# A hybrid layer with 32 experts on one core: expert weights as 2 MB pieces of a pair, in blocks of 4,096 columns, with 11 slots instead of 14

## The chip, the cores and the metric

The kernel runs on one core of a Trainium2 chip. The metric is device time in microseconds (us) of one execution; the time given is the median of several. The engines are TensorE (PE, its weight loads PEld), VectorE (DVE), ScalarE (ACT), GpSimd (POOL) and SyncE (SP); in this kernel SP issues all DMAs, and 16 DMA engines carry them out. TensorE's granted clock was 0.986 of full speed over the span.

## The reference

One layer over 256 tokens of width 1024, batch 1, all in float32. Four mixers of width 512 read one wide projection; then come the expert layer and the PLE branch, each with a layer norm after it.

```
z = x @ w_in                                  # zA, zB, zC, zD and the gates zG
yA, yB, yC, yD = rwkv7_mix(zA), hgrn2_mix(zB), mlstm_mix(zC), rglru_mix(zD)
merged = sum over n of sigmoid(zG)[n] * (y_n @ w_branch[n])
x = layernorm(alpha * x + merged @ w_out)
top_val, top_idx = top_k(x @ router_w + router_b, 4);  gate = softmax(top_val)
for each of the 32 experts, on its tokens:
    gu = x @ w_gu[e] + b_gu[e];  gate_, up = gu[:, :1024], gu[:, 1024:]       # clipped
    y  = ((up + 1) * gate_ * sigmoid(1.702 * gate_)) @ w_down[e] + b_down[e]
moe = sum of y * gate
ple = sigmoid(x @ ple_gate_w) * (p @ ple_proj_w)
out = layernorm(alpha * x + moe + ple)
```

The weights of the experts are 32 x (1024 x 2048 + 1024 x 1024) floats, 403 MB of the 475 MB that the kernel moves.

## The kernel before

The first 435 us (the front) hold the projection, the four mixers, the output projection, the first layer norm and the router. Then comes the expert stage: the experts are taken in 16 pairs, and both experts of a pair work in one product, each on one half of the 128 partitions of the output (64 tokens each). For pair `i`, `up(i)` makes the gate and up products (four of 1024 x 512 per expert), with bias, and the swiglu; `down(i, filler)` makes two products of 1024 x 512 per expert; `turn`, `gather`, `combine` and `down_bias` put the small products for transposing, for collecting the tokens of the next two pairs, for adding the result back and for the bias between them. After pairs 4 and 5 `ple(j)` makes one half of the PLE: the gate product with `w_pg` (32 products, L1868) and the projection with `w_pp` (8 products, L1878). Engines run in the order in which the program is written; nothing is reordered.

All weights come through one list, `stream`, in the order of use. `pump()` walks along it and issues as many DMAs on SP as places are free, `chunk()` hands a piece to the product that uses it, and `drop()` gives the place back and calls `pump()` again. A piece is 1 MB: 128 partitions x 2,048 floats, one run of 8,192 bytes per partition, for one expert. It lies in one of two kinds of place:

- a slot, 2,048 columns of its own (`Slots`, NSLOT = 14), used for other things in the front, too;
- a block of the arena (`Arena`, one wide tile of 22,208 columns, from which all other buffers are cut). `ar.blocks()` counts the free blocks of `B` columns (2,048); in the expert stage (`ar.tight`) large pieces start on block borders and small buffers avoid whole blocks.

The number of free places that must be left over is `st["keep"]`: 3, then `KEEP`, then 5 from the second pair on. A DMA that writes over a place waits for the last reader of what lay there, PE for weights; the wait stands on SP, and the DMAs behind it stand behind it. Up to eight DMAs are under way, since the program has eight DMA semaphores in turn. The last pieces of the last pair (`tails`) come in six DMAs with runs of 1,024 bytes or more, so that the end can start on parts.

The pair product, L1699 to L1710, and the lines of `pump()` that place a piece:

```
            if len(sl.idle) > st["slots"]:
                t = sl.get(F32)
                ...
            elif spare > (st["keep"] if st["slots"] else 0):
                ready[key] = al(shape)
```

Of the kernel before, what the change touches and what calls it, by code (L numbers as in the profile page):

```python
# [20 lines left out]
T = 256  # L21
# [106 lines left out]
class Arena:  # L128


    G, B = 32, 2048 // 32

    def __init__(self, t, cols):
        self.t, self.n = t, cols // self.G
        self.used = np.zeros(self.n, bool)
        self.freed = np.zeros(self.n, np.int64)
        self.now, self.live, self.peak, self.tight, self.low = 1, {}, 0, False, False

    def get(self, shape, dt=F32):
# [9 lines left out]
        if self.tight:  # L149
# [3 lines left out]
            else:  # L153
                whole = np.repeat(~self.used[:self.n // B * B].reshape(-1, B).any(axis=1), B)
                whole = np.append(whole, np.zeros(self.n - len(whole), bool))
                w = w + np.where(np.lib.stride_tricks.sliding_window_view(whole, g).any(axis=1), 1 << 40, 0)
        if self.low:
            w = np.where(w < 1 << 60, w >> 40 << 40, w) + np.arange(len(w))
# [43 lines left out]
NSLOT = 14  # L202
# [9 lines left out]
def hybrid_kernel(ctx: ExitStack, tc: tile.TileContext, xT, x, w_in, pc_d, rows_d, cn_d, lv_d, wa2, g2, lrub, w_br,  # L212
# [91 lines left out]
    st = {"next": 0, "out": 0, "ahead": 4, "slots": 1, "keep": 3}  # L304
    LATE = "br2_3"
    tails = [("dn", e, 512, 1) for e in (NE - 2, NE - 1)]

    def want(key, src, shape):
        stream.append((key, src, shape))

    def pump():
        while st["next"] < len(stream):
# [3 lines left out]
            if key in tails:  # L316
                if len(sl.idle) < len(tails):
                    break
                for key, _, shape in stream[st["next"]:]:
                    t = sl.get(F32)  # L320
                    place[key] = (sl.free, t)
                    ready[key] = in_slot(t, shape)
                for cc, k, n in ((0, 0, 4), (256, 0, 2), (256, 2, 2)):
                    for key, src, _ in stream[st["next"]:]:
                        src = src.rearrange("p (k c) -> p k c", k=4)
                        SY.dma_start(ready[key][:, k:k + n, cc:cc + 256], src[:, k:k + n, cc:cc + 256])
                st["next"] = len(stream)
                break
            spare = ar.blocks() if ar.tight else 0
            if st["slots"] == 0 and spare + len(sl.idle) <= st["keep"]:  # L330
                break
            if len(sl.idle) > st["slots"]:
                t = sl.get(F32)
                place[key] = (sl.free, t)
                ready[key] = in_slot(t, shape)
            elif spare > (st["keep"] if st["slots"] else 0):
                ready[key] = al(shape)
                place[key] = (fr, ready[key])
            elif late and st["out"] < 2:
                release(late.pop(0)[1])  # L340
                continue
            else:
                break
            if st["next"] == 0:
# [15 lines left out]
    def drop(key):  # L360
        f, t = place.pop(key)
        f(t)
# [227 lines left out]
    def rwkv():  # L590
# [56 lines left out]
        BK_t = sl.get(F32)  # L647
        BK = in_slot(BK_t, [128, 4, 512]).rearrange("p c (n i s) -> p c n i s", n=4, i=2)
        AR_t = sl.get(F32)
        AR = in_slot(AR_t, [128, 4, 512]).rearrange("p c (n i s) -> p c n i s", n=4, i=2)  # L650
# [77 lines left out]
        BKt_t = sl.get(F32)  # L728
        BKt = in_slot(BKt_t, [128, 4, 512])
# [35 lines left out]
        sl.free(BK_t)  # L765
# [144 lines left out]
        sl.free(AR_t)  # L910
        sl.free(BKt_t)
# [480 lines left out]
    def want_up(i):  # L1392
        for half in ((0, 0), (1, 0), (0, 1), (1, 1)):
            c0 = half[0] * D + half[1] * 512
            for k in range(2):
                for e in (2 * i, 2 * i + 1):
                    want(("gu", e, c0, k), w_gu[e, c0 // 512, k], [128, 4, 512])

    def want_down(i):
        for j in range(2):  # L1400
            for k in range(2):
                for e in (2 * i, 2 * i + 1):
                    want(("dn", e, j * 512, k), w_dn[e, j, k], [128, 4, 512])
        if i in PLE:
            j = PLE.index(i)
            for k in range(2):
                want(("pg", 0, j * 512, k), w_pg[j, k], [128, 4, 512])
# [10 lines left out]
    pump()  # L1418
    lz["pc"] = fetch(pc_d, [128, NPC])
    lz["half"] = al([128, 1])  # L1420
    G.memset(lz["half"], -0.5)
# [732 lines left out]
```

## Time and profile before

| | us |
|---|---|
| median of 3 runs | 1400.31 (1399.62 to 1402.27) |
| profiled execution | 1402.92 |
| its span, first to last instruction | 1400.5 |
| PE busy | 1294.5 (92 %) |
| DVE busy | 504.4 (36 %) |
| ACT busy | 330.6 (24 %) |
| DMA, mean over the span | 339 GB/s, 474.84 MB |

The rows further down come from the profiled execution. Times in them are us from the start of the span; L1705 is line 1705 of the kernel before. "slot", "arena" and "bank" are the names of places (a bank is an accumulator of PE), and in_w_gu, in_w_dn, in_w_pg, in_w_pp, in_w_in, in_w_br, in_w_out the weights in memory.

### The profile page before, as it was taken

Reading aid. Unit: us, or ns where it says so; the run is one execution under the profiler, and the core shown is the slowest. Engines: PE = TensorE matmul, PEld = TensorE weight load, DVE = VectorE, ACT = ScalarE, POOL = GpSimd, SP = SyncE. Lnnn points to the kernel's source line nnn. Section 1 sums busy time; section 2 is a strip of 40 time slices with the busy share of each in tenths; the row PEclk is TensorE's granted clock in tenths of the full one; section 3 lists DMA queues with packets and bytes.
Section 4 is the critical chain, followed back from the end, with each engine's and each line's share of the span. In section 5 each row is a group of like instructions: output and inputs, shape, how many; then the busy total and the mean of one; then the engine's idle time right before and its main releaser. Section 6 shows DMA issues by size and latency. Waiting matters only on the chain. (4 is left out here: it accounts for less than half of the span.)

```text
span 1400.5 us, 17423 instructions
## 1 busy us (share of the span) xinstructions
PE 1294.5 (92%) x7269; PEld 717.8 (51%) x7269; DVE 504.4 (36%) x715; ACT 330.6 (24%) x499; POOL 187.6 (13%) x197
## 2 busy tenths in 40 slices
PE   8988899999999998999889999989988898898985
PEld 8977879999994342333224333423433332342332
DVE  5887876686674122121121212201121211121114
ACT  6765654665433010010001000100100100010000
POOL 0578944413100000000000000000000000000000
PEclk9999999999999999999999999999999999999998
DMA  9413244458566999999999999999999999999995
GB/s 350 156 42 136 91 137 138 148 184 333 201 247 275 422 421 410 421 421 422 421 421 420 417 420 421 421 421 421 421 421 421 420 422 421 422 421 421 422 421 188
DMA packets 80151, 474.84 MB, mean 339 GB/s; under 512 B 14114, under 2 KB 20898, under 8 KB 24388
## 3 DMA queue, kind: packets, MB, share of 16 engines
q1 hardware_dynamic: 80068, 473.68, 83.7%
q8 instruction: 59, 0.97, 0.3%
q14 instruction: 24, 0.20, 0.0%
HBM read 472.07 MB, written 1.57 MB: 338 GB/s over the span
## 5 line engine op out<-in xcount | busy, mean ns | idle before, releaser
L1705 PE MATMUL bank<-slot,arena 128*64 128x512 f32 x2856 | 712.1, 600 | 58.1 <-DMA slot<-in_w_dn 32.1
L1705 PEld LDWEIGHTS bank<-slot,arena 128*64 128x64 f32 x2856 | 224.4, 137 | 460.7 <-issue 326.2
L378 PE MATMUL bank<-slot,slot 128*128 128x256 f32 (+2 forms) x800 | 243.9, 305 | 5.0 <-ACT slot L407 5.0
L379 PE MATMUL bank<-slot,slot 128*128 128x256 f32 (+2 forms) x800 | 239.6, 300 | 2.1 <-DVE slot L374 2.1
L380 PE MATMUL bank<-slot,slot 128*128 128x256 f32 (+2 forms) x800 | 239.7, 300 | 2.0 <-DVE slot L374 2.0
L378 PEld LDWEIGHTS bank<-slot,slot 128*128 128x128 f32 (+1 forms) x800 | 155.1, 194 | 11.7 <-ACT slot L407 5.0
L380 PEld LDWEIGHTS bank<-slot,slot 128*128 128x128 f32 (+1 forms) x800 | 155.1, 194 | 7.0 <-DVE slot L374 2.8
L379 PEld LDWEIGHTS bank<-slot,slot 128*128 128x128 f32 (+1 forms) x800 | 155.2, 194 | 6.2 <-DVE slot L374 2.5
L374 DVE TENSOR_TENSOR slot<-slot,slot 128x1024 fp32r<-128x1024 f32 (+1 forms) x89 | 123.8, 1399 | 47.8 <-ACT slot L373 47.6
L1695 DVE TENSOR_SCALAR arena<-bank 128x512 f32<-128x512 f32 x32 | 22.1, 692 | 236.9 <-PE bank L1705 230.1
L373 ACT CAST slot<-slot 128x1024 fp32r<-128x1024 f32 (+1 forms) x99 | 101.4, 1040 | 13.3 <-DVE slot L374 5.5
L1694 ACT ACTIVATE arena<-arena 128x512 f32<-128x512 f32 x32 | 20.2, 631 | 347.2 <-DVE arena L1693 347.2
L1716 DVE SCALAR_TENSOR_TENSOR slot<-bank,arena,slot 128x512 fp32r<-128x512 f32 (+1 forms) x33 | 24.2, 735 | 209.4 <-ACT slot L1715 209.1
L1581 POOL CAST se<-arena 128x128 fp32r<-128x128 f32 x16 | 5.0, 322 | 670.0 <-PE bank L1588 622.6
L1728 DVE TENSOR_TENSOR arena<-arena,bank 128x512 f32<-128x512 f32 (+1 forms) x66 | 40.1, 667 | 131.0 <-PE bank L1727 131.0
L1715 ACT ACTIVATE slot<-bank,arena 128x512 fp32r<-128x512 f32 (+1 forms) x33 | 22.3, 676 | 264.8 <-PE bank L1705 255.1
L1705 PE MATMUL bank<-arena 128*64 128x512 f32 x184 | 73.3, 599 | 5.4 <-DMA arena<-in_w_dn 2.7
L1693 DVE TENSOR_SCALAR arena<-bank 128x512 f32<-128x512 f32 x32 | 22.1, 689 | 120.6 <-PE bank L1705 120.6
L540 POOL TENSOR_TENSOR arena<-arena 128x4 f32<-128x4 f32 (+2 forms) x10 | 9.8, 990 | 354.7 <-DVE arena L2061 293.2
L1541 ACT ACTIVATE arena<-bank,arena 128x256 f32<-128x256 f32 x36 | 20.1, 566 | 114.1 <-DVE arena L1543 114.1
L1705 PEld LDWEIGHTS bank<-arena 128*64 128x64 f32 x184 | 21.0, 138 | 38.1 <-issue 26.8
L1794 ACT COPY arena<-bank 128x512 f32<-128x512 f32 x32 | 17.2, 590 | 92.3 <-PE bank L1793 92.3
(373 smaller groups left out, 1074.4 us busy)
## 6 DMA issues: line engine op xcount, KB each, us to landing
slot<-in_w_gu SPq DMA_DIRECT2D x237, 1024.0 KB, 18.6
slot<-in_w_dn SPq DMA_DIRECT2D x122, 1024.0 KB, 19.8
slot<-in_w_in SPq DMA_DIRECT2D x38, 1024.0 KB, 4.9
arena<-in_w_gu SPq DMA_DIRECT2D x19, 1024.0 KB, 16.0
slot<-in_w_br SPq DMA_DIRECT2D x7, 1024.0 KB, 4.9
slot<-in_w_pg SPq DMA_DIRECT2D x4, 1024.0 KB, 16.0
arena<-in_w_dn SPq DMA_DIRECT2D x4, 1024.0 KB, 19.9
arena<-in_w_in SPq DMA_DIRECT2D x3, 1024.0 KB, 7.7
```

What stands on the lines that cost most here:

```text
L373: S.copy(hi, src)
L374: (lo_eng or V).tensor_sub(lo, src, hi)
L378: PE.matmul(o, a[0], b[0], start=first, stop=False)
L379: PE.matmul(o, a[0], b[1], start=False, stop=False)
L380: PE.matmul(o, a[1], b[0], start=False, stop=last)
L1693: V.tensor_scalar_min(g_, pg[0], 7.0)
L1694: S.activation(s_, g_, AF.Sigmoid, scale=1.702)
L1695: V.tensor_scalar(u_, pg[1], -7.0, 7.0, op0=ALU.max, op1=ALU.min)
L1705: PE.matmul(p[64 * a:64 * a + 64], lhs(a, k), chunk(kind, ex[a], c0, k // 4)[:, k % 4], start=b0 is None and k == 0, stop=k == KT - 1)
L1715: S.activation(y[:, 0], p, AF.Copy, scale=w)
L1716: V.scalar_tensor_tensor(y[:, 1], p, w, y[:, 0], op0=ALU.mult, op1=ALU.subtract)
L1728: V.tensor_add(moe[t][:, o:o + n], moe[t][:, o:o + n], p[:, 0:n])
```

## The change

The weights of a pair lie side by side in memory (`chunks()`), so that a pair's piece is one DMA of 2 MB: 128 partitions, one run of 16,384 bytes each. A block of the arena has 4,096 columns, and the arena grows from 22,208 to 28,352 columns, since NSLOT goes from 14 to 11. `two()` places such a piece: in a block, or, while slots may be used up, as two halves of 1 MB in two slots. The product of a pair gives its piece back at once (`prod`), the gate product of the PLE its 2 MB after all eight steps instead of 1 MB after each four (`ple`). The condition that leaves places over counts a block as two, and `keep` is 6 from the second pair on. In the front, the pieces of `w_in`, `w_br` and `w_out` go to the arena first (`one()`), and BK, AR, BKt of the RWKV mixer lie in the arena instead of in slots; three buffers of constants are put at the arena's high end (`ar.high`). The y buffer of the expert stage is taken when it is first used (`st["hold"]`). The products, and the order of the instructions on PE, DVE, ACT and POOL, are the same; SP issues 317 DMAs instead of 504.

```diff
-    G, B = 32, 2048 // 32
+    G, B = 32, 4096 // 32
...
-NSLOT = 14
+NSLOT = 11
...
+    def one(key, src, shape):
+        if not ar.tight:
+            t = ar.get(shape)
+            if t is not None:
+                placed(key, [t], fr)
+                ready[key] = t
+                return True
+        if len(sl.idle) > st["slots"]:
...
+    def two(key, src):
+        spare, idle = ar.blocks(), len(sl.idle) - st["hold"]
+        if st["slots"] == 0 and 2 * spare + idle <= st["keep"] + 1:
+            return False
+        if spare > (0 if st["slots"] == 0 else st["keep"] // 2):
+            t = al([128, 2, 4, 512])
+            placed(key, [t], fr)
+            ready[key] = t[:, 0], t[:, 1]
+            if key != TAIL:
+                SY.dma_start(t.rearrange("p e k c -> p (e k c)"), src.rearrange("p e f -> p (e f)"))
+            return True
+        if idle >= st["slots"] + 2:
+            ts = [sl.get(F32) for a in range(2)]
+            placed(key, ts, sl.free)
+            ready[key] = [in_slot(t, [128, 4, 512]) for t in ts]
+            if key != TAIL:
+                for a in range(2):
+                    SY.dma_start(ts[a][:, 0:2048], src[:, a])
+            return True
+        return False
...
-        BK_t = sl.get(F32)
+        BK_t = al([128, 4, 512])
...
-                for e in (2 * i, 2 * i + 1):
-                    want(("gu", e, c0, k), w_gu[e, c0 // 512, k], [128, 4, 512])
+                want(("gu", i, c0, k), w_gu[i, c0 // 512, k], None)
...
-                PE.matmul(p[64 * a:64 * a + 64], lhs(a, k), chunk(kind, ex[a], c0, k // 4)[:, k % 4],
+                PE.matmul(p[64 * a:64 * a + 64], lhs(a, k), chunk(kind, i, c0, k // 4)[a][:, k % 4],
                           start=b0 is None and k == 0, stop=k == KT - 1)
             if k % 4 == 3:
-                for a in range(2):
-                    drop((kind, ex[a], c0, k // 4))
-                    pump()
+                drop((kind, i, c0, k // 4))
+                pump()
...
-            st["keep"] = 5
+            st["keep"] = 6
...
-            if k % 4 == 3:
-                drop(("pg", 0, j * 512, k // 4))
-                pump()
+        drop(("pg", 0, j * 512))
+        pump()
...
-        return f(a.reshape(e, r // 512, 4, 128, c // 512, 512).transpose(0, 4, 1, 3, 2, 5)).reshape(
-            e, c // 512, r // 512, 128, 2048)
+        return f(a.reshape(e // 2, 2, r // 512, 4, 128, c // 512, 512).transpose(0, 5, 2, 4, 1, 3, 6)).reshape(
+            e // 2, c // 512, r // 512, 128, 2, 2048)
```

What the order of the instructions makes of it is shown at three places. In these rows a number behind `slot` is the slot and the one behind the underscore a running number, and the brackets hold what the DMA waits for: PE or DVE (the last reader of the place), and one of the eight DMA semaphores DMAHW0 to 7.

SP at the start of the expert stage, before:

```order
L356 DMA arena_58<-in_w_gu 128x2048 [waits DMAHW1_49]
L356 DMA arena_58<-in_w_gu 128x2048 [waits DMAHW2_49,PE_49]
L356 DMA slot12_4457<-in_w_gu 128x2048 [waits DMAHW3_49,PE_49]
L356 DMA slot8_4459<-in_w_gu 128x2048 [waits DMAHW4_49,PE_49]
L356 DMA slot11_4469<-in_w_gu 128x2048 [waits DMAHW5_49,PE_49]
L356 DMA slot10_4479<-in_w_gu 128x2048 [waits DMAHW6_49,PE_49]
L356 DMA arena_58<-in_w_gu 128x2048 [waits DMAHW7_49]
L356 DMA slot3_4498<-in_w_gu 128x2048 [waits DMAHW0_49,PE_49]
L356 DMA slot2_4500<-in_w_gu 128x2048 [waits DMAHW1_49,PE_49]
L356 DMA slot0_4510<-in_w_gu 128x2048 [waits DMAHW2_49,PE_49]
L356 DMA slot1_4512<-in_w_gu 128x2048 [waits DMAHW3_49,PE_49]
L356 DMA slot4_4523<-in_w_gu 128x2048 [waits DMAHW4_49,PE_49]
```

Each row is one piece of one expert, and two rows next to each other are a pair. After, from the same place of the stage, a row in the arena is a whole pair:

```order
L348 DMA arena_58<-in_w_gu 128x4096 [waits DMAHW7_49,PE_49]
L348 DMA arena_58<-in_w_gu 128x4096 [waits DMAHW0_49,PE_49]
L348 DMA arena_58<-in_w_gu 128x4096 [waits DMAHW1_49,PE_49]
L348 DMA arena_58<-in_w_gu 128x4096 [waits DMAHW2_49,PE_49]
L356 DMA slot7_4468<-in_w_gu 128x2048 [waits DMAHW3_49]
L356 DMA slot10_4469<-in_w_gu 128x2048 [waits DMAHW4_49]
L356 DMA slot2_4480<-in_w_gu 128x2048 [waits DMAHW5_49,PE_49]
L356 DMA slot0_4481<-in_w_gu 128x2048 [waits DMAHW6_49,PE_49]
L348 DMA arena_58<-in_w_gu 128x4096 [waits DMAHW7_49,PE_49]
L348 DMA arena_58<-in_w_gu 128x4096 [waits DMAHW0_49,PE_49]
L348 DMA arena_58<-in_w_dn 128x4096 [waits DMAHW1_49,PE_49]
L348 DMA arena_58<-in_w_dn 128x4096 [waits DMAHW2_49,PE_49]
```

Before, pieces go round ten slots (12, 8, 11, 10, 3, 2, 0, 1, 4, 13), with a block of the arena now and then. After, the first 2 MB pieces lie in the arena, two more pairs of 1 MB take slots, and from there on each piece is one DMA into the arena, which waits for PE.

SP around the first product of the PLE, before:

```order
L356 DMA slot3_5586<-in_w_dn 128x2048 [waits DMAHW1_49,PE_49]
L356 DMA slot2_5597<-in_w_dn 128x2048 [waits DMAHW2_49,PE_49]
L356 DMA slot0_5599<-in_w_dn 128x2048 [waits DMAHW3_49,PE_49]
L356 DMA slot1_5609<-in_w_pg 128x2048 [waits DMAHW4_49,PE_49]
L356 DMA slot4_5611<-in_w_pg 128x2048 [waits DMAHW5_49,PE_49]
L356 DMA slot13_5627<-in_w_pp 128x1024 [waits DMAHW6_49,PE_49]
L356 DMA slot12_5629<-in_w_gu 128x2048 [waits DMAHW7_49,PE_49]
L356 DMA slot8_5702<-in_w_gu 128x2048 [waits DMAHW0_49,PE_49]
L356 DMA slot11_5704<-in_w_gu 128x2048 [waits DMAHW1_49,PE_49]
L356 DMA slot10_5717<-in_w_gu 128x2048 [waits DMAHW2_49,PE_49]
```

Here w_pg comes in two pieces with a slot each, given back one by one. After, it is one:

```order
L348 DMA arena_58<-in_w_dn 128x4096 [waits DMAHW0_49,PE_49]
L348 DMA arena_58<-in_w_dn 128x4096 [waits DMAHW1_49,PE_49]
L348 DMA arena_58<-in_w_pg 128x4096 [waits DMAHW2_49,PE_49]
L389 DMA slot3_5414<-in_w_pp 128x1024
L348 DMA arena_58<-in_w_gu 128x4096 [waits DMAHW3_49,PE_49]
L348 DMA arena_58<-in_w_gu 128x4096 [waits DMAHW4_49,PE_49]
L348 DMA arena_58<-in_w_gu 128x4096 [waits DMAHW5_49,PE_49]
L348 DMA arena_58<-in_w_gu 128x4096 [waits DMAHW6_49,PE_49]
L348 DMA arena_58<-in_w_gu 128x4096 [waits DMAHW0_49,PE_49]
L348 DMA arena_58<-in_w_gu 128x4096 [waits DMAHW1_49,PE_49]
```

The piece of w_pg has moved into the arena, with the pieces behind it, whose blocks come round; w_pp lies in a slot and waits for nothing.

ACT in the front, in the mixers HGRN2 (L927, L959 after) and RWKV (the rest), before:

```order
L994 ACTIVATE arena_58<-arena_58 128x16x32 [waits DVE_49]
L373 CAST slot8_1327<-slot6_1098 128x1024
L927 ACTIVATE arena_58<-bank2_1103 128x512 [waits DVE_49,PE_49,Pool_49]
L927 ACTIVATE arena_58<-bank5_1104 128x512 [waits PE_49]
L737 COPY slot9_1166<-bank4_1363 128x512 [waits PE_49]
L747 COPY slot7_1374<-bank6_1369 64x512 [waits PE_49,Activation_49]
```

Here L927 waits for PE, and for DVE and POOL. After, the same instructions:

```order
L1026 ACTIVATE slot4_1287<-arena_58 128x16x32 [waits DVE_49]
L407 CAST slot8_1312<-arena_58 128x1024
L959 ACTIVATE arena_58<-bank2_1086 128x512 [waits DVE_49]
L959 ACTIVATE arena_58<-bank5_1087 128x512
L770 COPY arena_58<-bank4_1348 128x512 [waits PE_49]
L780 COPY arena_58<-bank6_1354 64x512 [waits PE_49]
```

The order is the same, but the activation in L959 now stands behind DVE alone: its place in the arena is one that held a w_in piece, of which DVE reads the last part.

## Rows read from the trace of the kernel before

**Rows 1.** The page's 40 slices of the span (35 us each): busy tenths of PE, busy tenths of the DMA engines, GB/s that they moved.

```profile
PE   8988899999999998999889999989988898898985
...
DMA  9413244458566999999999999999999999999995
GB/s 350 156 42 136 91 137 138 148 184 333 201 247 275 422 421 410 421 421 422 421 421 420 417 420 421 421 421 421 421 421 421 420 422 421 422 421 421 422 421 188
```

**Rows 2.** Busy time by stage. Columns: the stretch in us, its length, busy us and instructions of PE, PEld, DVE, ACT and POOL, granted clock, DMA share, GB/s.

```profile
433.00:460.00 27.00, 27.00 (x144) 11.54 (x144) 6.55 (x15) 4.66 (x7) 0.00 (x0) 0.96 0.64 247
460.00:1365.00 905.00, 841.81 (x3680) 318.86 (x3679) 168.41 (x274) 81.04 (x136) 3.90 (x14) 0.99 1.01 421
```

**Rows 3.** The order in time of PE in the steady part of the expert stage: start us, length us, engine, line, operation, output from inputs, count, and in brackets the idle time ahead and what ended it. One row is a pair piece.

```profile
559.73 3.65 PE L1705 MATMUL bank<-slot,arena 128*64 128x512 f32 x16 [1.32 <-DMA slot<-in_w_dn]
564.69 3.65 PE L1705 MATMUL bank<-slot,arena 128*64 128x512 f32 x16 [1.31 <-DMA slot<-in_w_dn]
```

**Rows 4.** The page's DMA issues: what, queue, count, KB each, median us from issue to landing.

```profile
slot<-in_w_gu SPq DMA_DIRECT2D x237, 1024.0 KB, 18.6
slot<-in_w_dn SPq DMA_DIRECT2D x122, 1024.0 KB, 19.8
slot<-in_w_in SPq DMA_DIRECT2D x38, 1024.0 KB, 4.9
```

**Rows 5.** The DMAs of in_w_gu that were issued in three stretches (628 to 640 us, 771 to 790, 835 to 860): their first and last start, and the time to landing.

```profile
L356 SPq DMA_DIRECT2D slot<-in_w_gu x4: 328/356/383, 633.3 to 637.1; - x4
...
DMA to landing us min/median/max: 8.4/10.1/12.0
...
L356 SPq DMA_DIRECT2D slot<-in_w_gu x7: 327/328/384, 771.5 to 786.6; - x7
...
DMA to landing us min/median/max: 8.2/9.7/10.6
...
L356 SPq DMA_DIRECT2D slot<-in_w_gu x6: 327/328/384, 837.0 to 851.7; - x6
...
DMA to landing us min/median/max: 10.0/11.3/13.4
```

**Rows 6.** The order in time of PE at the gather of 501 us, and at the bias product and the gather of 613 to 630 us.

```profile
501.37 4.11 PE L1660 MATMUL bank<-oh,slot 128*128 128x256 f32 x32
...
506.58 5.79 PE L1705 MATMUL bank<-slot,arena 128*64 128x512 f32 x26
...
613.00 0.39 PE L1739 MATMUL bank<-arena 128*32 128x128 f32 x2
...
619.02 5.44 PE L1705 MATMUL bank<-slot,arena 128*64 128x512 f32 x16
624.40 4.09 PE L1660 MATMUL bank<-oh,slot 128*128 128x256 f32 x32
...
629.60 4.93 PE L1705 MATMUL bank<-slot,arena 128*64 128x512 f32 x22
```

**Rows 7.** The order in time of PE at the first product of the PLE.

```profile
754.02 14.00 PE L1868 MATMUL bank<-slot,arena 128*128 128x512 f32 x32
767.86 3.60 PE L1878 MATMUL bank<-slot,arena 128*128 128x512 f32 x8
771.38 0.50 PE L1588 MATMUL bank<-slot,se 64*128 64x512 f32 x1
```

**Rows 8.** The order in time of PE at the start of the expert stage.

```profile
434.45 3.87 PE L1705 MATMUL bank<-arena 128*64 128x512 f32 x16
438.25 2.18 PE L1660 MATMUL bank<-oh,slot 128*128 128x256 f32 x16
...
441.54 7.07 PE L1705 MATMUL bank<-slot,arena 128*64 128x512 f32 x32
```

**Rows 9.** What the DMA queues moved in four stretches, 351.5 to 353.5 us (w_out, runs of 4,096 B), 421 to 431 us and 640 to 730 us (expert weights, runs of 8,192 B), 1378 to 1381 us (the last pieces, runs of 1,024 B). First all packets, their MB, the rate and how many were short; then, for all but the second, the share of the 16 engines' time that the packets of this queue took.

```profile
DMA packets 222, 0.84 MB, mean 422 GB/s; under 512 B 16, under 2 KB 16, under 8 KB 222
...
q1 hardware_dynamic: 222, 0.84, 102.8%
...
DMA packets 584, 4.26 MB, mean 426 GB/s; under 512 B 64, under 2 KB 64, under 8 KB 64
...
DMA packets 5200, 37.90 MB, mean 421 GB/s; under 512 B 577, under 2 KB 577, under 8 KB 577
...
q1 hardware_dynamic: 5197, 37.85, 101.1%
...
DMA packets 550, 0.54 MB, mean 182 GB/s; under 512 B 33, under 2 KB 549, under 8 KB 549
...
q1 hardware_dynamic: 549, 0.53, 51.5%
```

**Rows 10.** The order in time of ACT, of DVE and of PE around 132 to 145 us, and of PE at 429 us.

```profile
132.77 1.09 ACT L927 ACTIVATE arena<-bank 128x512 f32<-128x512 f32 x2
135.06 0.59 ACT L737 COPY slot<-bank 128x512 f32<-128x512 f32 x1 [1.20 <-PE bank L736]
...
137.57 1.32 DVE L374 TENSOR_TENSOR slot<-slot,slot 128x1024 fp32r<-128x1024 f32 x1
...
143.99 0.69 PE L1005 MATMUL bank<-slot 128*64 128x64 f32 x16 [2.63 <-DVE slot L1000]
...
429.73 0.37 PE L1622 MATMUL bank<-mk,rsup 128*128 128x32 f32 x2 [0.88 <-DVE arena L1625]
```

More of the change, by code (lines that the diff above doesn't have):

```diff
@@ L303, in hybrid_kernel, with placed @@
     stream, place, ready = [], {}, {}
-    st = {"next": 0, "out": 0, "ahead": 4, "slots": 1, "keep": 3}
+    st = {"next": 0, "out": 0, "ahead": 4, "slots": 1, "keep": 3, "hold": 0}
     LATE = "br2_3"
-    tails = [("dn", e, 512, 1) for e in (NE - 2, NE - 1)]
+    TAIL = ("dn", NE // 2 - 1, 512, 1)
     def want(key, src, shape):
         stream.append((key, src, shape))
+    def placed(key, tiles, back):
+        place[key] = back, tiles
+    def one(key, src, shape):
[6 more added lines that the diff above has]
+        if len(sl.idle) > st["slots"]:
+            t = sl.get(F32)
+            placed(key, [t], sl.free)
+            ready[key] = in_slot(t, shape)
+            return True
+        if ar.tight and 2 * ar.blocks() > st["keep"]:
+            t = al(shape)
+            placed(key, [t], fr)
+            ready[key] = t
+            return True
[6 more added lines that the diff above has]
+            t = al([128, 2, 4, 512])
+            placed(key, [t], fr)
+            ready[key] = t[:, 0], t[:, 1]
+            if key != TAIL:
+                SY.dma_start(t.rearrange("p e k c -> p (e k c)"), src.rearrange("p e f -> p (e f)"))
+            return True
+        if idle >= st["slots"] + 2:
[5 more added lines that the diff above has]
+                    SY.dma_start(ts[a][:, 0:2048], src[:, a])
+            return True
+        return False
     def pump():
@@ L315, in pump @@
                 break
[L316 to L322, printed above, removed]
-                for cc, k, n in ((0, 0, 4), (256, 0, 2), (256, 2, 2)):
[L324 to L344, printed above, removed]
+            if not (two(key, src) if shape is None else one(key, src, shape)):
+                if late and st["out"] < 2:
+                    release(late.pop(0)[1])
+                    continue
+                break
+            if key == TAIL:
+                for cc, k, n in ((0, 0, 4), (256, 0, 2), (256, 2, 2)):
+                    for a in range(2):
+                        w = src[:, a].rearrange("p (k c) -> p k c", k=4)
+                        SY.dma_start(ready[key][a][:, k:k + n, cc:cc + 256], w[:, k:k + n, cc:cc + 256])
+            elif shape is None:
+                pass
+            elif st["next"] == 0:
                 src = src.rearrange("p (k c) -> p k c", k=KT)
@@ L360, in drop @@
     def drop(key):
-        f, t = place.pop(key)
-        f(t)
+        back, tiles = place.pop(key)
+        for t in tiles:
+            back(t)
         del ready[key]
@@ L909, in rwkv @@
             yield
-        sl.free(AR_t)
-        sl.free(BKt_t)
+        fr(AR_t, BKt)
         fr(state, YT, eLc, *MR, *VS)
@@ L1718, in new_rest @@
     def new_rest():
+        if not ybuf:
+            st["hold"] = 0
+            y_t = sl.get(F32R)
+            ybuf.extend(in_slot(y_t, [128, 4, 512])[:, 2 * i:2 * i + 2] for i in range(2))
         ybuf.append(ybuf.pop(0))
@@ L1987, in overflows @@
         done_with(*ob)
-    ybuf = [in_slot(y_t, [128, 4, 512])[:, 2 * i:2 * i + 2] for i in range(2)]
+    ybuf = []
+    st["hold"] = 1
     first = gather(0)
```

48 lines of the change are left out of this document (27 added, 21 removed).

## The prediction, made before the run

> **What bounds it now.** I read the page's slices first, then the busy time by stage, the waits of the DMA queue, and last the order in time of TensorE (PE) around each wait. The slices [rows 1] show two kernels in one span: up to about 435 us the DMA engines are half idle and PE is busy eight or nine tenths; from slice 14 on the DMA moves 421 GB/s in almost every slice. The windows say it more sharply [rows 2]: from 460 to 1365 us the DMA share is 1.01, the rate 421 GB/s, while PE has 93 % and waits: each pair of pieces (2 MB) costs PE 3.65 us, starts every 4.96 to 4.97 us and stands 1.3 us idle "<-DMA" before it [rows 3]. 1 MB lands in half of 4.97, 2.487 us, which is 1,048,576 B at 421 GB/s. So in the expert stage the last landing sets the end, and the rest (end of PE, the six tail DMAs, layer norm, output) follows it as now. Two things can move that landing: the **rate** at which a landing follows the one before, and stretches in which the **queue is empty** since no buffer is free.
>
> How near the queue is to empty is told by issue to landing. A DMA with nothing ahead of it takes 4.8 to 4.9 us [rows 4]; less 2.49 of transfer this is about 2.4 us before its bytes flow. In the expert stage the median is 18.6 and 19.8 us: six or so pieces stand ahead. It sinks to 8.2 us after the first gate product of the PLE, 10.0 after the second, 8.4 after the gather at 624 to 630 us [rows 5]. It never comes near 4.9: 3.3 us of queue are left at the worst place, and the 14 slots just suffice.
>
> **What the change does, part by part.**
>
> *Depth.* In the order before, pieces go round ten slots and now and then an arena block, 10 to 12 MB. After, the expert weights go round four blocks of 4,096 columns, 8 MB; the condition of `two()` (2 x blocks + idle slots must exceed keep + 1 = 7) leaves seven slots idle, so a piece's DMA waits for PE's last product on the piece four before it. In steady state PE is done 3.6 us after a landing; three pieces (14.9 us) are then under way, and the next must be issued 2.4 us before they are through: at 12.5 us after the landing. PE may be late by 12.5 - 3.6 = 8.9 us. The gather (5.2 us, 501.37 to 506.58) and the bias product with the gather behind it (6.0 and 5.2 us, 613.00 to 619.02 and 624.40 to 629.60, with pairs between them that each give 1.4 back) [rows 6] pass under that.
>
> The gate product does not: it holds its block for the whole of L1868, 14.0 us, since both halves are now given back together, and L1878 follows, 3.6 us [rows 7]. PE comes to it about 1.5 us late, from the gather. The piece that takes its block may be issued at 12.5 + 1.2 (the 0.5 MB of w_pp, half of 2.487) = 13.7 us, and is at 14.0 + 1.5 = 15.5: 1.8 us empty (1.5 in the recurrence below). The next waits for the first pair after L1878: PE is done with it at 17.4 + 0.4 + 3.6 + 1.5 = 22.9, and the queue wanted it at 20.5: 2.4 us. The third costs 0.5 (a turn of 1.0 us stands in between). That is 4.5 for each of the two products, **9 us**.
>
> At the start of the stage the queue is dry already: 433 to 460 us has share 0.64 [rows 2], so 27 x (1 - 0.64/1.01) = 9.9 us empty. After, 16 MB instead of 15 wait in SBUF, but then the frees of PE set the pace: first pair done at 438.3, the next ones 3.5 us apart [rows 8]. The queue is empty 8.9 us to the first DMA, then 1.5 and 2.5 us at the second and third (the third takes the block of the fourth pair), and 2.3 and 0.8 at 495 and 511 us where slots give way to blocks: 16.0 - 9.9 - 2.5 (the MB that is in already) = 3.6, **4 us**.
>
> I carried both buffer orders through all 194 pieces by landing(n) = max(landing(n-1), issue(n) + 2.4) + c, issue = PE's end on the piece whose buffer it takes, PE's end = max(its last end, landing) + 3.5 and the extra products. At c = 4.974 for both, the last landing comes **13.1 us later**.
>
> *Rate.* The gain is that a packet is 16,384 B instead of 8,192. Its fixed part is read from busy time per packet [rows 9]: 16 engines x 90 us x 1.011 over 4,623 packets of 8 KB is 315.1 ns; 32.9 us over 206 packets of 4 KB (the w_out burst) 159.7 ns; 24.7 us over 516 packets of 1 KB (the tail) 47.9 ns. Two 4 KB packets less one of 8 KB give 4.3 ns fixed, the line from 1 to 8 KB gives 9.7. One packet for two saves half of that per 8 KB: 0.7 to 1.5 %. The short packets (577 beside the 4,623, one per engine and DMA) halve too. I take 1.2 %: c = 4.915. In the recurrence 1 % of rate is worth about 8 us, not the 9.3 of the plain stretch of 930 us, because a faster DMA is starved longer in the same places. So -59 ns x 0.16 us per ns = **-9.4 us**. The ends: nothing at all, since the 4 KB burst ran at 422 GB/s and 8 KB at 421 (only the share differs, 1.028 to 1.011), which is c = 4.974; and 2 % (all of the 9.7 ns and the short packets, with as much again for gaps between DMAs), c = 4.875, **-16 us**. The burst of 421 to 431 us at 426 GB/s, 1.2 % over the steady rate with the same packets [rows 9], shows that 421 is no ceiling.
>
> The Trainium skill ("DMA: Bandwidth & Descriptors", section "Why small descriptors are slow (HBM only)") gives a packet about 3 cycles beside one per 32 B, 3 in 259 here; by that the saving would be 0.6 %, and the end 9.0 us later instead of the 4.2 of my sum. The 4.3 ns of the row are nearest to it.
>
> *The front.* The buffers BK, AR and BKt, the w_in pieces and the constants change their places there. The worst new wait that I found is ACT's L927 at 132.77 us, which now writes over the columns of a piece that DVE still reads in L374 at 137.57, to 138.89 [rows 10]: 6.1 us late. Behind it on ACT stand L737, L747, L993 for PE's L1005, which sits idle 2.63 us before 143.99 as it is, and PE waits again 0.88 us before 429.73. Two more such waits, shorter, lie at about 75 and 243 us. Bounds: 0 and 6.1; I take **0.5**, since the stage's start at 434.45 hangs on a chain with idle time in it. SP issues 317 instead of 504 DMAs, which shortens nothing that is waited for. The tail keeps its six DMAs: 0.
>
> Sum: 13.1 - 9.4 + 0.5 = +4.2. The profiled execution took 1402.92 us (span 1400.5), the median is 1400.31; against the median this is **1404.5 us**. A measurement of this kernel tells 0.2 %, 2.8 us, from no change.
>
> **Rivals.**
> - *The rate gives all, or more* (the other side). From 2 % of rate on (c at or below 4.872, since (13.1 + 0.5 + 2.8) / 0.16 is 102 ns) the stage gains more than the empty places cost: c = 4.85 gives -6.2, c = 4.82 gives -11, so 1389 to 1397 us. For it: the 1 KB line and 426 GB/s in the burst. Against: 4 to 8 KB shows 4.3 ns only. Beside it stands a page: the Trainium skill, same page, section "Where 436 GB/s comes from", has a ceiling of 435 GB/s, 3 % above the row; the highest row here is 426. Chance of faster by over 0.2 %: 0.24.
> - *The rate gives nothing.* The engines are limited by bytes, as 4 KB at 422 and 8 KB at 421 say. Then +13.1 and 0.5: 1413 to 1414. Chance 0.14.
> - *The front's wait is not covered*: 6.1 instead of 0.5 on top of the sum: 1410. For it: PE is busy eight or nine tenths up to 435 us [rows 1]; against: the idle times above. Chance 0.07.
> - *No difference*: 1.35 to 2 % of rate (c from 4.907 to 4.872), within 2.8 us either way, 1398 to 1403. Chance 0.25.
> - My own forecast, 0.6 to 1.35 % of rate, +2.8 to +9: 0.30.
>
> **Numbers.** Faster 0.24, same 0.25, slower 0.14 + 0.07 + 0.30 = 0.51. The range goes from 2.5 % of rate to no gain at all: 1394 to 1414; outside stay the front's wait on top of a poor rate and half of the first rival, 0.16. The likeliest case's own range is 1403 to 1409.
>
> **What would show it.** In the steady stretch PE starts a pair every 4.91 to 4.92 us and the rate is near 426 GB/s; 4.97 is the second rival, 4.88 the first. The DMA share falls below 1 at 765 to 795 and 835 to 865 us, some 4 to 5 us empty in each, with SP waiting for PE's L1868 (L1904 of the changed kernel) and for the pair after it. 433 to 515 us has some 6 us more empty than now, with 1 MB more landed ahead of it. PE reaches its first pair within 1 us of 434.45. The forecast is wrong if the queue is never empty at the gate products, if the rate in the steady stretch is not 1 to 1.5 % up, or if the stage begins late.

## The result

The changed kernel takes 1415.43 us (median of 6 runs, 1409.65 to 1422.26) against 1400.33 us before: ratio 1.0106, 95 % interval 1.0074 to 1.0138, 15 us slower. That is above the range (1394 to 1414) and 11 us above the forecast of 1404.5. The profiled execution took 1416.04 us with a span of 1414.2 us, 13.7 us more than before; the account below is made between these two spans. One of the twelve executions of a run further down (five pieces deep, with both waits) took 1796.14 us at a granted clock of 0.652; the time given for that run is the median of the other eleven.

### The profile page after: what moved, and what is told of

It reads as the page before. It is cut to its first block, busy times and chain, and to the rows that moved or that the text cites. A ratio compares the mean times of both kernels' runs of the same rounds, so it can differ in the third digit from the quotient of the medians.

```text
span 1414.2 us, 17062 instructions
## 1 busy us (share of the span) xinstructions
PE 1267.3 (90%) x7269; PEld 699.6 (49%) x7269; DVE 504.7 (36%) x715; ACT 329.1 (23%) x499; POOL 184.0 (13%) x197
## 5 line engine op out<-in xcount | busy, mean ns | idle before, releaser
L1738 PE MATMUL bank<-arena 128*64 128x512 f32 x2816 | 639.6, 599 | 91.7 <-DMA arena<-in_w_gu 52.6
L1738 PEld LDWEIGHTS bank<-arena 128*64 128x64 f32 x2816 | 193.7, 137 | 483.0 <-issue 328.1
L408 DVE TENSOR_TENSOR slot<-arena,slot 128x1024 fp32r<-128x1024 f32 (+1 forms) x69 | 97.0, 1419 | 24.1 <-ACT slot L407 23.9
L407 ACT CAST slot<-arena 128x1024 fp32r<-128x1024 f32 (+1 forms) x75 | 75.8, 1035 | 3.2 <-DMA arena<-in_w_in 2.3
L408 DVE TENSOR_TENSOR slot<-slot,slot 128x1024 fp32r<-128x1024 f32 x30 | 40.2, 1341 | 34.2 <-ACT slot L407 34.2
L1692 PEld LDWEIGHTS bank<-oh,slot 128*128 128x128 f32 x256 | 32.4, 198 | 7.2 <-issue 5.7
L1763 PE MATMUL bank<-slot,slot 128*128 128x512 f32 (+1 forms) x132 | 35.1, 402 | 0.7 <-ACTq L2012 0.6
```

Source lines behind the costliest of these rows:

```text
L407: S.copy(hi, src)
L408: (lo_eng or V).tensor_sub(lo, src, hi)
L1692: PE.matmul(p[:, j * 256:j * 256 + 256], x1s[t][1 + i][:, k * 128:k * 128 + 128], flat(oh[:, t]), start=t == 0 and i == 0, stop=t == 1 and ...
L1738: PE.matmul(p[64 * a:64 * a + 64], lhs(a, k), chunk(kind, i, c0, k // 4)[a][:, k % 4], start=b0 is None and k == 0, stop=k == KT - 1)
L1763: PE.matmul(p[:, 0:n], ow[0][:, half, t], y[:, i], start=i == 0, stop=i == 1)
```

## The profile of the changed kernel

The slices of the page, as in [rows 1], with PE's granted clock in tenths:

```profile
PEclk9999899999999999989999999999999999999998
DMA  9413252463787999999999998999999999999994
GB/s 347 153 48 129 90 165 105 149 236 127 285 333 270 415 377 415 428 396 377 428 429 426 359 429 343 429 427 428 428 427 427 429 428 428 428 427 428 427 428 184
```

Where the DMA is not held up it now moves 428 GB/s instead of 421, so the longer run does what it says, and by more than forecast: in the steady part PE starts pairs at 1104.32, 1109.22, 1114.10 and 1119.00 us, one every 4.89 us. Beside that there are holes (slices at 377, 396, 377, 359 and 343), where the kernel before has no slice of the expert stage below 410 but the last. The same by stage, in the columns of [rows 2]; the first two stretches are the start of the expert stage, then the bias product with the gather, the two gate products of the PLE, and a stretch without any of them:

```profile
433.00:460.00 27.00, 25.68 (x147) 13.92 (x147) 8.80 (x28) 8.48 (x14) 0.00 (x0) 0.94 0.67 252
460.00:515.00 55.00, 55.00 (x283) 21.33 (x279) 11.89 (x22) 5.70 (x10) 0.82 (x3) 1.00 0.95 397
620.00:660.00 40.00, 38.08 (x172) 16.64 (x173) 9.44 (x18) 5.55 (x10) 0.00 (x0) 0.87 0.88 354
765.00:795.00 30.00, 30.00 (x100) 12.71 (x100) 6.59 (x10) 2.93 (x6) 0.00 (x0) 1.00 0.91 360
835.00:865.00 30.00, 28.66 (x94) 12.48 (x94) 5.44 (x9) 2.95 (x5) 0.00 (x0) 1.00 0.88 348
900.00:1200.00 300.00, 258.04 (x1194) 92.56 (x1192) 52.96 (x85) 24.70 (x41) 1.30 (x5) 1.00 1.01 428
```

Counted in bytes, a stretch at less than 428 GB/s has lost its length times (1 - rate / 428): 6.9 us at the bias product and the gather, 4.8 and 5.6 us at the gate products. (By the DMA share, 0.91 and 0.88 against 1.01, it would be 3.0 and 3.9 us at the gate products. The account here goes by bytes, since they decide when the last piece lands.) Before, these three stretches moved 422, 415 and 421 GB/s.

How much later each place is reached is read from PE's order in time. First pair of the expert stage, bias product and gather, first and second gate product, first of the last pieces:

```profile
440.99 3.87 PE L1738 MATMUL bank<-arena 128*64 128x512 f32 x16
...
619.28 0.39 PE L1775 MATMUL bank<-arena 128*32 128x128 f32 x2
621.92 6.78 PE L1781 MATMUL bank<-arena 32*128 32x512 f32 x8 [2.24 <-ACT arena L1776]
...
634.17 4.10 PE L1692 MATMUL bank<-oh,slot 128*128 128x256 f32 x32
...
764.72 13.97 PE L1904 MATMUL bank<-arena 128*128 128x512 f32 x32 [0.29 <-DMA arena<-in_w_pg]
...
836.36 13.97 PE L1904 MATMUL bank<-arena 128*128 128x512 f32 x32 [1.34 <-DMA arena<-in_w_pg]
...
1389.96 3.67 PE L1798 MATMUL bank<-arena 128*64 128x256 f32 x32 [1.48 <-DMA arena<-in_w_dn]
```

Against the kernel before that is +6.5 us at the first pair (434.45 in [rows 8]), +6.3 at the bias product and +9.8 at the gather (613.00 and 624.40 in [rows 6]), +10.7 at the first gate product (754.02 in [rows 7]), +16.8 at the second and +13.1 at the last pieces (before, the two rows below). The second gate product starves the pieces behind it once more, 5.6 us, and then the better rate gives some 9 us back over 550 us.

```profile
819.54 14.00 PE L1868 MATMUL bank<-slot,arena 128*128 128x512 f32 x32
...
1376.89 3.67 PE L1762 MATMUL bank<-slot,arena 128*64 128x256 f32 x30 [1.24 <-DMA slot<-in_w_dn]
```

So three things need a cause: 6.5 us that are lost before the expert stage begins, the bias product that takes 9.3 us (619.28 to 628.62) instead of 6.0, and the holes. For the first, ACT and PE around 140 us, and the stretches there (columns as above):

```profile
138.35 1.09 ACT L959 ACTIVATE arena<-bank 128x512 f32<-128x512 f32 x2 [6.07 <-DVE slot L408]
```

```profile
145.16 1.12 PE L1037 MATMUL bank<-arena 128*64 128x64 f32 x16 [4.35 <-DVE arena L1032]
```

```profile
140.00:145.00 5.00, 0.81 (x7) 0.60 (x6) 2.65 (x3) 4.69 (x8) 3.67 (x4) 0.95 0.00 0
145.00:150.00 5.00, 4.84 (x33) 4.75 (x34) 4.16 (x4) 2.53 (x4) 4.69 (x8) 0.50 0.00 0
160.00:165.00 5.00, 2.96 (x12) 2.67 (x13) 3.42 (x6) 3.48 (x6) 4.29 (x10) 0.66 0.64 211
```

ACT stands 6.07 us in L959, as predicted from the order; PE's idle time ahead of L1037 grows from 2.63 to 4.35 us; and then the granted clock is 0.50 for 145 to 150 us and 0.66 for 160 to 165 us, where before it was 0.68 and 1.00:

```profile
145.00:150.00 5.00, 5.00 (x33) 5.00 (x32) 3.43 (x5) 4.01 (x7) 4.84 (x6) 0.68 0.09 38
160.00:165.00 5.00, 5.00 (x37) 4.43 (x37) 4.89 (x8) 3.72 (x7) 4.53 (x7) 1.00 0.52 165
```

Most of the delay enters later than L1037. At 155 us PE is only 0.9 us later than before (L1043 at 154.37 before, the same product, L1075, at 155.23 after). Then it waits again, for a cast that ACT makes late, and works at the clock of 0.66; at 167.47 us it is 6.3 us behind (161.16 before):

```profile
161.53 0.58 PE L412 MATMUL bank<-slot,slot 128*128 128x256 f32 x1 [2.30 <-ACT slot L407]
```

## The experiments

The theory after this profile: two waits on places that are still being read (L959 in the front, L1776 ahead of the bias product) and a ring of four pieces that is too shallow for the gate products together cost more than the rate gives. The rivals: the ring alone decides, and what is gained ahead of a hole is lost in it; or the rate comes from something else than the run's length.

**One wait at a time.** `AGE` is the number of frees after which the arena takes a place as old; it changes which places are reused, and with them the waits; the program is otherwise the same.

```diff
-AGE = 13
+AGE = 7
```

> The changed kernel, with one number of the arena's choice of places altered (a place counts as old after 7 frees instead of 13). By the order of the waits this gives ACT's L959 a place that nobody reads any more, so its wait of 6.07 us at 132 us is gone; the ring of four blocks and the wait of L1776 at the bias product stay. Theory A (that wait leaves PE idle 4.35 us at 141 to 145 us, the granted clock then falls to 0.50 in 145 to 150 us and 0.66 in 160 to 170 us, and all of it, 6.5 us, reaches the expert stage): PE starts its first pair within 2 us of 434.5 instead of 440.99, the clock of 140 to 175 us is back at 0.95, and the time falls by 5 to 7 us, to about 1409. Theory B (the start of the stage is late for another reason, or the queue at the start of the stage takes the delay up again): less than 2 us.

1408.63 us, ratio 1.0056 (1.0043 to 1.0068): 6.8 us won. PE starts the expert stage at 435.58, and behind L959's place the clock is back:

```profile
140.00:145.00 5.00, 3.98 (x38) 3.73 (x38) 4.11 (x4) 2.82 (x5) 4.76 (x6) 0.84 0.00 0
145.00:150.00 5.00, 3.96 (x34) 3.76 (x34) 3.41 (x6) 4.01 (x8) 4.76 (x7) 1.00 0.18 28
```

```profile
245.01 1.16 PE L908 MATMUL bank<-arena 128*128 128x128 f32 x8 [1.40 <-ACT arena L899]
...
435.58 3.65 PE L1738 MATMUL bank<-arena 128*64 128x512 f32 x16
```

Theory A, near its number: 5.4 of the 6.5 us go with this wait. The other 1.1 us are still there. They enter at 245 us, where PE stands 1.40 us ahead of L908 in this run and 1.45 us in the changed kernel, and not at all before: one of the two shorter waits that the prediction names at 75 and 243 us.

```diff
-AGE = 13
+AGE = 18
```

> The changed kernel with the same number at 18: by the order of the waits L959's wait stays, and the copy L1776 ahead of the bias product gets a free place, so PE does not stand 2.24 us before it. The ring stays at four blocks. Theory A (the wait and the low clock behind it make the bias product 9.3 us instead of 6.0 and push PE over the 8.9 us that four blocks allow): the queue is empty 3 us less between 628 and 660 us and the time falls by 3 to 5 us, to about 1411. Theory B (the bias product and the gather behind it overrun the ring anyway): PE's idle time there is gone, the queue is as empty as before, the time stays within 1.5 us of 1415.

1409.91 us, ratio 1.0056 (1.0039 to 1.0074): 5.5 us won, a little more than expected. The size is uncertain: the executions lie between 1402.16 and 1413.68 us, and the shorter wait at 243 us goes with this number, too. The bias product takes 4.5 us instead of 9.3, the clock stays at 1.00, and the hole of 6.9 us in 620 to 660 us is all but gone (0.6 us):

```profile
619.89 0.40 PE L1775 MATMUL bank<-arena 128*32 128x128 f32 x2
620.73 3.70 PE L1781 MATMUL bank<-arena 32*128 32x512 f32 x8 [0.45 <-ACT arena L1776]
624.36 3.65 PE L1738 MATMUL bank<-arena 128*64 128x512 f32 x16
```

```profile
620.00:660.00 40.00, 39.55 (x202) 17.50 (x203) 12.23 (x21) 6.17 (x11) 0.00 (x0) 1.00 1.00 422
```

Not all of this is the wait. It is 1.8 us longer in the changed kernel than before (2.24 against 0.45 us ahead of the eight products); the rest is the clock, which fell at this place in the kernel before, too (5.25 us for the eight products there, 6.78 in the changed kernel, 3.70 here).

**Both waits.** `AGE` 18, and the buffer that L959 writes in a slot:

```diff
-                Z[name] = al([128, 2, 512])
+                if name == "hg":
+                    hg_t.append(sl.get(F32))
+                    Z[name] = in_slot(hg_t[0], [128, 2, 512])
+                else:
+                    Z[name] = al([128, 2, 512])
...
-        fr(Z["hg"])
+        sl.free(hg_t[0])
```

> The changed kernel without either wait: the number at 18, and the buffer hg of the mixer HGRN2, which L959 writes, in a slot of its own. Theory A: both gains, about 10 us, so 1404 to 1406: what is left over the kernel before is the empty queue at the two gate products (10 us) and at the start of the stage (4 us), less 15 us of rate and plus about 3 us of starvation behind the gathers. Theory B (the ring alone decides, and what PE gains ahead is lost at the next empty place): 1411 to 1415.

1404.6 us, ratio 1.0027 (1.0018 to 1.0036): 10.8 us won, nearly the sum of the two (12.3). What is left are the holes of the ring. At the gate products they are as large as ever, 5.7 and 6.3 us. At the bias product and the gather 3.2 us are left, though PE waits no longer for L1776; the clock falls again there, and the pair behind the bias product takes 6.03 us:

```profile
610.34 3.65 PE L1744 MATMUL bank<-arena 128*64 128x512 f32 x16 [1.25 <-DMA arena<-in_w_gu]
...
614.76 4.67 PE L1787 MATMUL bank<-arena 32*128 32x512 f32 x8 [0.45 <-ACT arena L1782]
619.36 6.03 PE L1744 MATMUL bank<-arena,slot 128*64 128x512 f32 x16
...
630.51 10.06 PE L1744 MATMUL bank<-arena,slot 128*64 128x512 f32 x45
```

```profile
620.00:660.00 40.00, 40.00 (x203) 17.06 (x201) 8.57 (x17) 5.81 (x10) 0.00 (x0) 0.95 0.95 394
765.00:795.00 30.00, 30.00 (x119) 11.74 (x119) 7.82 (x12) 2.90 (x5) 0.00 (x0) 1.00 0.89 347
835.00:865.00 30.00, 30.00 (x116) 11.89 (x116) 7.82 (x12) 2.90 (x5) 0.00 (x0) 1.00 0.87 338
```

**The depth.** The kernel without the two waits, with one number changed (then 2 instead of 4 for six deep):

```diff
-            st["keep"] = 6
+            st["keep"] = 4
```

> The kernel without the two waits (1404.6), with keep 4 instead of 6 from the second pair on: a fifth piece of a pair goes into two of the idle slots, as two DMAs of 1 MB with runs of 8,192 bytes. Theory A (depth: what is left over is the queue running empty where PE is more than 8.9 us late): with five pieces the allowance grows to some 13.8 us, the queue stays full at both gate products (DMA share 1.0 at 765 to 795 and 835 to 865 us instead of 0.87 to 0.89), and one piece in five at the old rate costs 0.3 %, 2 to 3 us: 1396 to 1399. Theory B (the empty queue at the gate products is paid back by PE, which is the later one there): 1404 to 1407.

1390.57 us, ratio 0.9924 (0.9911 to 0.9937): another 14 us, and 10 us under the kernel before. That is 5 us better than expected. The gate products leave only a small hole (403 and 405 GB/s, 1.7 and 1.5 us at 427), the gather none:

```profile
460.00:515.00 55.00, 55.00 (x281) 21.56 (x281) 12.01 (x22) 6.38 (x11) 0.82 (x3) 1.00 1.00 417
620.00:660.00 40.00, 39.98 (x204) 16.20 (x203) 8.86 (x16) 5.81 (x10) 0.00 (x0) 1.00 1.01 427
765.00:795.00 30.00, 30.00 (x132) 10.85 (x132) 8.50 (x13) 2.33 (x4) 0.29 (x1) 1.00 1.00 403
835.00:865.00 30.00, 30.00 (x139) 10.88 (x137) 5.94 (x10) 2.33 (x4) 0.29 (x1) 1.00 0.99 405
900.00:1200.00 300.00, 263.50 (x1187) 94.92 (x1185) 53.68 (x87) 23.99 (x40) 1.30 (x5) 1.00 1.01 427
```

One piece in five in slots, with short runs, costs 1 GB/s, not the 0.3 % and 2 to 3 us that were set down for it.

> The same with keep 2: six pieces deep, two of six in slots with runs of 8,192 bytes. If five pieces are enough, the sixth only lowers the rate by another 0.2 % (4.921 instead of 4.911 us a pair): 1 to 2 us slower than five deep, 1398 to 1400. If five are not enough at the gate products, it is faster than five deep.

1392.49 us, ratio 0.9939 (0.9926 to 0.9952): the same within the intervals. Five pieces are enough.

> The changed kernel with both waits and keep 4: five pieces deep, the fifth in two slots. Depth alone: the gate products (10 us in the lateness against the kernel before) and the bias product with the gather (5 us) no longer empty the queue, one piece in five is at the old rate (2 to 3 us): the time falls by 10 to 13 us from 1415 to 1402 to 1405, and the 6 to 7 us of the front stay. If the empty places hide in one another, less than 6 us.

1399.61 us (changed kernel, keep 4), ratio 0.9982 (0.9967 to 0.9997): 16 us won by depth alone, with both waits in place, more than the 10 to 13 expected. The holes do not hide in one another.

> The kernel without the two waits, four blocks deep, with the gate weights as two pieces of 1 MB in idle slots, each given back after its four steps. If the block that the gate product holds for 14.0 us is what empties the queue (as the prediction says of the first 1.8 us of each), the time falls by 3 to 4 us. If it is only that PE comes 17.4 us later to the pieces behind, which fill the four blocks by then, the queue is empty about as long, at one place instead of three: the time falls by no more than 1.5 us, 1403 to 1405.

```diff
-            want(("pg", 0, j * 512), w_pg[j], None)
+            for k in range(2):
+                want(("pg", 0, j * 512, k), w_pg[j][:, k], [128, 4, 512])
...
-        drop(("pg", 0, j * 512))
-        pump()
+            if k % 4 == 3:
+                drop(("pg", 0, j * 512, k // 4))
+                pump()
```

1403.47 us, ratio 1.002 (1.0008 to 1.0031), 1.1 us under the kernel without waits, within what the intervals leave open. The holes at the gate products shrink a little, to 5.0 and 3.9 us from 5.7 and 6.3:

```profile
765.00:795.00 30.00, 30.00 (x123) 11.48 (x123) 7.82 (x12) 2.90 (x5) 0.00 (x0) 1.00 0.89 356
835.00:865.00 30.00, 30.00 (x124) 11.33 (x125) 7.83 (x12) 2.90 (x5) 0.00 (x0) 1.00 0.93 373
```

So about a quarter of these holes, 3.1 of 12.0 us in the profiled executions, goes with the block that w_pg holds, which the prediction named first; whether the time gains as much is left open by the intervals. The larger part stays: the four blocks are full of pieces that PE comes to 17.4 us late, and five pieces remove it.

**The rate.** The ring of the changed kernel, with runs of 8,192 bytes, once as two DMAs of 1 MB into a block and once as one DMA of 2 MB (the halves one behind the other in memory, those of w_pg alike):

```diff
-                SY.dma_start(t.rearrange("p e k c -> p (e k c)"), src.rearrange("p e f -> p (e f)"))
+                for a in range(2):
+                    SY.dma_start(t[:, a].rearrange("p k c -> p (k c)"), src[:, a])
```

> The changed kernel, with each block filled by two DMAs of 1 MB with runs of 8,192 bytes (8 packets of 8 KB instead of 8 of 16 KB per engine) in the same ring. If the run's length makes the rate (1.6 % more: a pair lands every 4.895 us instead of 4.974), the rate falls back to 421 GB/s, a pair takes 4.97 us, and the time rises by 9 to 13 us to 1424 to 1428, less than the 15 us of the plain stretch since a slower queue is starved less. If the rate comes from fewer DMAs in flight or from the places, it stays at 428 GB/s and 1415.

1422.02 us, ratio 1.0143 (1.012 to 1.0166): 6.6 us slower than the changed kernel, where 9 to 13 were expected; the holes at the gate products are smaller (373 and 386 GB/s), as a slower queue is starved less. The intervals of the two times overlap (1.0074 to 1.0138 for the changed kernel); what decides is the steady stretch, which is back at 421 GB/s.

```diff
-                SY.dma_start(t.rearrange("p e k c -> p (e k c)"), src.rearrange("p e f -> p (e f)"))
+                SY.dma_start(t.rearrange("p e k c -> p e (k c)"), src.rearrange("e p f -> p e f"))
...
-        return f(a.reshape(e // 2, 2, r // 512, 4, 128, c // 512, 512).transpose(0, 5, 2, 4, 1, 3, 6)).reshape(
-            e // 2, c // 512, r // 512, 128, 2, 2048)
+        return f(a.reshape(e // 2, 2, r // 512, 4, 128, c // 512, 512).transpose(0, 5, 2, 1, 4, 3, 6)).reshape(
+            e // 2, c // 512, r // 512, 2, 128, 2048)
```

> The changed kernel, with the two experts' halves one after the other in memory, so that a block is filled by one DMA of 2 MB whose runs are 8,192 bytes (two per partition). It separates what the run of the two halves changed together: the length of the run and the number of DMAs. If the run's length makes the rate, the steady stretch (900 to 1200 us) moves 421 GB/s, as with two DMAs. If the number of DMAs does (a short packet per engine and DMA, and the gaps between DMAs), it moves 427 to 428.

1426.97 us in one run. What the DMA queues moved in 1000 to 1100 us (columns as in [rows 9]), for the changed kernel, then with two DMAs, then with one:

```profile
DMA packets 2933, 42.78 MB, mean 428 GB/s; under 512 B 322, under 2 KB 322, under 8 KB 322
```

```profile
DMA packets 5779, 42.13 MB, mean 421 GB/s; under 512 B 639, under 2 KB 639, under 8 KB 639
```

```profile
DMA packets 5460, 42.12 MB, mean 421 GB/s; under 512 B 321, under 2 KB 321, under 8 KB 321
```

One DMA for two halves the short packets, 639 to 321, and moves nothing faster. So it is the run's length that makes the 428 GB/s, not the number of DMAs.

**All in blocks.** Fewer slots give the arena a fifth block for weights (`NSLOT` 9, `keep` 4, nothing else):

> The changed kernel with NSLOT 9 (the arena has 32,448 columns then) and keep 4: by the order, five blocks go round, each filled by one DMA of 2 MB with runs of 16,384 bytes; ACT's L959 has a free place and waits for nothing; the copy L1776 ahead of the bias product still waits for DVE. If depth and rate are the whole account, the queue is full at the gate products as five deep, and every piece lands in 4.895 us instead of one in five at 4.974: 2 to 3 us under five deep (1390.6), so 1387 to 1389, less what the smaller lead at the start (fewer slots to load ahead) takes back, 1 to 3 us. If 2 MB pieces in five blocks behave otherwise than the mix: 1391 or more.

1393.1 us, ratio 0.9941 (0.9927 to 0.9955): above what was expected, and no better than five deep; the two profiled executions take 1393.1 and 1392.98 us. The steady rate is 428 GB/s. With fewer slots less is loaded ahead, 79.6 MB by 433 us against 81.8 five deep, but by 515 us it is 111.4 against 111.6, so only half a microsecond of that is left; and the wait of L1776 is still there. As far as a run can tell that differs in these two things as well, it matters little what the fifth piece lies in; that it is there is worth 14 us.

## Why the prediction was wrong

- **The front, the step that failed most.** It was put at 0.5 us, between 0 and 6.1, "since the stage's start at 434.45 hangs on a chain with idle time in it". It cost 6.5 us, more than the upper bound: 5.4 go with L959's wait, and the run without it is 6.8 us faster; 1.1 come in at the wait at 243 us. The wait, its length and its place were right, the cover was wrong. At L1037 (L1005 before) the chain did swallow most of it: PE's idle time grew from 2.63 to 4.35 us, 1.7 of the 6.07. But those 2.63 us were idle because PE already waited for that same chain, so they are no cover; and what follows was not looked at, the 2.30 us for ACT at 161 us and the products at a clock of 0.50 to 0.66. The rival "not covered" had this case at 0.07.
- **The bias product and the gather, put at nothing.** They were said to pass under the allowance of 8.9 us, "with pairs between them that each give 1.4 back". The rows do not say that. There is one pair between them, and it took 5.44 us, longer than a landing, so it gives nothing back. PE began the pair ahead of the bias product as it landed, at 609.42; two landings later it is 619.37; PE came to that pair at 629.60, 10.2 us late. So four blocks are overrun with the lengths of before, and the kernel without the two waits shows it: 610.34 plus two landings is 620.13, PE comes at 630.51, 10.4 us late, and 3.2 us are lost. In the changed kernel a wait that was not found comes on top: 2.24 us for a copy (L1776, onto a place that DVE's L1729 reads), and then the low clock. That makes 9.3 us of the bias product and 6.9 us of the hole. The prediction looked for new waits of this kind in the front only.

```profile
609.42 3.65 PE L1705 MATMUL bank<-slot,arena 128*64 128x512 f32 x14 [1.33 <-DMA slot<-in_w_gu]
```

- **The gate products, mis-sized.** 9 us were forecast, 10.4 us are in the two stretches of the changed kernel and 12.0 in those of the kernel without waits. The sum was made at 4.974 us a piece and for a PE that is 1.5 us late; that this is the difference is not shown. The held block, the first part of the sum, is worth about a quarter at most; the depth of four was right, since a fifth piece leaves 3.2 of the 12.0 us.
- **The start of the stage.** 16.0 us of empty queue from 433 to 515 us were forecast; 27 x (1 - 252 / 428) + 55 x (1 - 397 / 428) is 15.1, and 16.3 in the kernel without waits (255 and 386 GB/s). Right. The 9.9 us of before go by the DMA share; by bytes they are 11.2. The 1 MB more landed ahead is there only without the waits, as 0.8 MB; in the changed kernel, with its late front, 1.3 MB less had moved by 433 us. Without the waits the term is then 16.3 - 11.2 - 1.8 (0.8 MB) = 3.3, where 3.6 was taken.
- **The rate, mis-sized the other way.** 428 instead of 421 GB/s is 1.6 %, 4.895 us a pair; 1.2 % was taken, with 0.7 to 1.5 % from the rows and 2 % as the end. In the sum this is 3 us too little gain. Per packet saved, 8 packets of 16 KB take 4.895 us on each engine and 16 of 8 KB 4.974: 2 x 310.9 - 611.9 = 9.9 ns, the value of the line from 1 to 8 KB (9.7), not the 4.3 of the nearest rows. (From the shown figures the 315.1 ns of that working come out as 314.9, which makes 4.5 of the 4.3 and moves no bound.) The reason that was given for "nearest", the 4 KB burst, was weaker than it looked: 2 us of data, with rates and shares to three digits. The rule of the Trainium skill's "DMA: Bandwidth & Descriptors" ("Why small descriptors are slow (HBM only)"), 3 cycles a packet and so an estimate of 0.6 %, does not fit this trace: the gain is 1.6 %.
- **The second rival** ("the rate gives nothing", 1413 to 1414) comes out nearest in time, by luck, and is wrong in every step: the rate gave more than forecast, and the waits ate it.

Taken together: the terms for depth and rate alone made +3.7; the kernel without the two waits measures +3.8 against its own runs of before (1404.6 against 1400.78). That is luck: the holes cost more than forecast (3.2 us at the bias product and gather, 3.0 at the gate products), and the rate gave more. What the forecast lacked beyond that is the 10.8 us of the waits.

In the profiled executions the account closes within a microsecond or so. What the DMA queues had moved by 433 us, before and after:

```profile
DMA packets 23620, 80.81 MB, mean 187 GB/s; under 512 B 7968, under 2 KB 12704, under 8 KB 15392
```

```profile
DMA packets 22853, 79.50 MB, mean 184 GB/s; under 512 B 7872, under 2 KB 12608, under 8 KB 15296
```

The 1.3 MB are 3.1 us. Then 433 to 515 us lose 15.1 us against 11.2 before, which is 3.9; in these two the late front shows, and it must not be added a second time. The bias product and the gather lose 6.9, the gate products 10.4, and smaller stretches between 515 and 900 us 3.0 more than before (419 GB/s at 515 to 620 and 795 to 835 us, 411 at 865 to 900). The 186 pieces that are not in SBUF when the stage begins land 0.079 us sooner each, 14.7 less. The sum is 12.6 us; PE comes to the last pieces 13.1 us later, and the span is 13.7 us longer.

## What to carry to other kernels

When buffers are moved to pay for a better transfer, count the waits on reused places for every instruction that moves, in all stages, and do not set idle time of the engine behind them against their length where that engine idles for the same chain: that idle time grows with it. Count what the reader does between two pieces from the rows, pair by pair. A ring must be as deep as the longest time its reader is away, and a piece in a poor place beats no piece: here one piece in five at the old run length cost 1 GB/s and brought 14 us. The longer run was worth having (1390.6 us against 1400.9) once the two waits were gone and the idle slots were used.

## What the runs showed of the hardware

The granted clock goes with a wait's price. Behind the 6 us of L959's wait, with PE idle 4.35 us, it was 0.50 at 145 to 150 us, the lower of the two levels (1.2 GHz against 2.4), and it fell again behind the wait at 161 us. At 160 to 170 us it was 0.58 in the run that kept this wait and lost only the one at the bias product, and 1.00 in the run without L959's wait:

```profile
160.00:170.00 10.00, 8.22 (x31) 6.88 (x32) 8.82 (x14) 7.06 (x11) 7.95 (x15) 0.58 0.23 93
```

```profile
160.00:170.00 10.00, 10.00 (x83) 8.74 (x81) 9.75 (x19) 6.43 (x10) 8.98 (x15) 1.00 0.21 84
```

The changed kernel's times spread over 12.6 us (1409.65 to 1422.26). The spread goes with L959's wait: in the four kernels that were run several times and keep it, it is 10.5 to 12.6 us, in the six without it 2.7 to 5.7 us. The longest and the shortest time of the changed kernel have the lowest and the highest mean clock (0.979 and 0.985), but between them the order is not kept (1411.92 us at 0.981, 1414.82 at 0.984). That the clock makes the spread is what these numbers suggest; no run sets it by itself. The bias product shows at one place what the clock costs: eight products took 5.25 us before and 6.78 after, and 3.70 us where the clock stayed at 1.00.
